# Own trigger points and a sixth buffer for the loads of summed weight tiles

## The chip, the core and the metric

The kernel runs on one core of one Trainium2 chip. The metric is the device time of one launch in microseconds (us). The engines are named as in the profile: PE is TensorE, DVE is VectorE, ACT is ScalarE, POOL is GpSimd and SP is SyncE; PEld is the weight load of PE. A "q" behind an engine (SPq) marks its queue of instructions.

## What is computed

The reference is a decoder trunk of two layers on a sequence of 512 tokens of width 1024. The change concerns the MLP at the end of each layer:

```python
h2 = rms_norm(x, norm2_g[l])
x = x + jnp.square(jax.nn.relu(h2 @ w_up[l])) @ w_down[l]
```

`w_up` is 1024 x 4096 and `w_down` is 4096 x 1024, both float32. In front of it, each layer has a gated recurrence, a windowed attention in three groups and an output projection, which the change doesn't touch.

## The kernel before

**Weights.** All weights of a layer lie in one array of 148 tiles of 128 x 1024 float32 (512 KB), in the order of their use. Each tile is loaded and split into a high part `wH` (ACT, line 112) and the rest `wL` (DVE, line 113), and a product takes three matmuls: high by high, high by low, low by high. `plan` (line 54) writes the list of the tiles in the order of their products. `weight` (line 123) keeps three split tiles in a queue: before it hands one out it calls `prep` (line 81) for the tile two places further on. `prep` runs at high priority. `wH` and `wL` have three buffers each, so a split waits until the product of three tiles before is done. The framework orders each engine's instructions when the program is compiled, and that order is then fixed; semaphores hold an instruction back until its data and its buffer are there.

**The MLP.** For each quarter of the 4096 inner columns (q = 0 to 3), `up` (line 667) computes eight products with plain ("raw") tiles, of 24 matmuls of 512 columns each; `operands` (line 599) then forms seven combinations of the squared results. The product with `w_down` is done by `seven` (line 610) in two groups (g = 0, 1) per quarter. A group replaces eight products of blocks by seven, whose weights are sums of blocks. So a layer has eight groups and the kernel sixteen; each has seven tiles of 24 matmuls of 256 columns (line 631), 168 in all. The first product of the next quarter stands ahead of group 0, its other seven behind group 1, so that the two groups of a quarter follow each other without a pause. After each product `take` adds the accumulator to `x` on DVE (line 638), and later products of the group write the same accumulator again.

**The tiles of a group.** `groups` in `plan` lists seven items. With w0 to w3 for the four blocks:

- x11: f11 = w0, a plain load; split
- s1: f1 = w2, a load on SP (line 104), to which a DMA of POOL then adds w3 in place (line 105); split
- s2: f2 = f1 + f11, an addition on DVE (line 107); split
- s4: f12 = w1, a load (line 110), and f4 = f2 + f12 on DVE (line 111); split
- s3: f3 = w0, a load, to which POOL adds w2 in place; split
- x12: f12 again; split
- raw: w3, a load into the buffers of the raw tiles; split

The tiles f11, f1, f2, f4, f12 and f3 share one tag "f" with five buffers. The buffers go round in the order in which the tiles are made in the program: the n-th tile takes the buffer of the tile five places earlier and waits until that one has been read for the last time. A load is part of `prep` of its own item.

Of the kernel before, what the change touches and what calls it, by code (L numbers as in the profile page):

```python
# [8 lines left out]
F32 = mybir.dt.float32  # L9
# [3 lines left out]
OP = mybir.AluOpType  # L13

P = 128
S = 512
D = 1024
KD = 8
# [5 lines left out]
NW = 148  # L24
# [4 lines left out]
class Trunk:  # L29
# [24 lines left out]
    def plan(self):  # L54
        items = []
        for l in range(DEPTH):
            at = l * NW
            plain = lambda n: [("raw", l, at - l * NW + i) for i in range(n)]

            def take(n):  # L60
                nonlocal at
                got = plain(n)
                at += n
                return got

            def groups():
                nonlocal at
                got = []
                for g in range(2):
                    i = at - l * NW  # L70
                    got += [("x11", l, i), ("s1", l, i + 2, i + 3), ("s2",), ("s4", l, i + 1),
                            ("s3", l, i, i + 2), ("x12",), ("raw", l, i + 3)]
                    at += 4
                return got

            items += take(NW - 64 + KD + 1) + groups()
            for q in (1, 2):
                items += take(KD) + groups()
            items += take(KD - 1) + groups()
        self.items = items  # L80

    def sum_tile(self):
        return self.mp.tile([P, 1024], F32, tag="f", name=self.nm("f"), bufs=5)

    def prep(self, urgent=True):
        nc = self.nc
        kind, *at = self.items[self.wi]
        self.wi += 1
        with self.tc.high_priority() if urgent else nullcontext():
            if kind == "x12":  # L90
                raw = self.f12
            elif kind == "raw":
                raw = self.wp.tile([P, 1024], F32, tag="raw", name=self.nm("raw"), bufs=2)
            else:
                raw = self.sum_tile()
            h = self.wp.tile([P, 1024], F32R, tag="wH", name=self.nm("wH"), bufs=3)
            lo = self.wp.tile([P, 1024], F32R, tag="wL", name=self.nm("wL"), bufs=3)
            n = 1024 // self.parts
            for c in range(self.parts):
                cs = slice(c * n, (c + 1) * n)  # L100
                if kind in ("raw", "x11"):
                    nc.sync.dma_start(raw[:, cs], self.w[at[0], at[1], :, cs])
                elif kind in ("s1", "s3"):
                    nc.sync.dma_start(raw, self.w[at[0], at[1]])
                    nc.gpsimd.dma_start(raw, self.w[at[0], at[2]], accum_op=OP.add)
                elif kind == "s2":
                    nc.vector.tensor_add(raw, self.f1, self.f11)
                elif kind == "s4":
                    self.f12 = self.sum_tile()
                    nc.sync.dma_start(self.f12, self.w[at[0], at[1]])  # L110
                    nc.vector.tensor_add(raw, self.f2, self.f12)
                nc.scalar.activation(h[:, cs], raw[:, cs], AF.Copy)  # L112
                nc.vector.tensor_sub(lo[:, cs], raw[:, cs], h[:, cs].bitcast(F32))  # L113
            self.parts = 1
        if kind == "x11":
            self.f11 = raw
        elif kind == "s1":
            self.f1 = raw
        elif kind == "s2":
            self.f2 = raw  # L120
        self.wq.append((h, lo))

    def weight(self):
# [584 lines left out]
    def finish(self, x, xp, cs):  # L708
        nc = self.nc
        bc = self.bcast(self.stats([self.ssq[:, cs], self.sq]))  # L710
        rb = xp.tile([P, 256], F32, tag="rbf", name=self.nm("rbf"), bufs=2)
        nc.scalar.activation(rb, bc, AF.Copy)
        for k in range(KD):
            if k < 2:
                nc.gpsimd.tensor_mul(x[:, k, cs], x[:, k, cs], rb)
            else:
                nc.vector.tensor_mul(x[:, k, cs], x[:, k, cs], bc)
        for a, b in ((2, 4), (4, 6), (0, 2), (6, 8)):
            (nc.sync if a % 4 else nc.scalar).dma_start(self.outT[a:b, :, cs].rearrange("k p t -> p k t"), x[:, a:b, cs])
# [19 lines left out]
    def run(self):  # L739
        nc, tc = self.nc, self.tc  # L740
        with ExitStack() as es:
# [4 lines left out]
            self.mm = es.enter_context(tc.tile_pool(name="mmps", bufs=4, space=bass.MemoryType.PSUM))  # L746
            self.ax = es.enter_context(tc.tile_pool(name="axps", bufs=2, space=bass.MemoryType.PSUM))
            self.hx = es.enter_context(tc.tile_pool(name="hxps", bufs=2, space=bass.MemoryType.PSUM))
            self.wi, self.wq, self.parts = 0, [], 4
            self.plan()  # L750

            def open_x(name):
                xs = ExitStack()
                xp = xs.enter_context(tc.tile_pool(name=name, bufs=1, side="right", reuse_waits="tile"))
                return xp.tile([P, KD, S], F32, name=name + "_t"), xp, xs
# [5 lines left out]
            x, xp, xs = open_x("x_in")  # L761
# [39 lines left out]
            for l in range(DEPTH):  # L801
                with ExitStack() as ms:
                    pool = lambda st, name, bufs, side="left": st.enter_context(tc.tile_pool(
                        name=f"{name}{l}", bufs=bufs, side=side, reuse_waits="tile"))
# [45 lines left out]
                    x, xp, xs = open_x(f"x{l}")  # L850
# [11 lines left out]
                    rb = xp.tile([P, S], F32, name=self.nm("rb"))  # L862
# [127 lines left out]
```

## Time and profile before

| | |
|---|---|
| runs shown | 1811.43, 1815.75, 1817.28 us; median 1815.75 |
| profiled execution | 1819.03 us, of which the span from the first to the last instruction is 1817.1 |
| busy in the span | PE 98%, PEld 84%, DVE 62%, ACT 40%, POOL 5% |
| granted clock of PE | mean 0.992 of full speed |
| DMA | 199 MB, mean 110 GB/s |

The profile is of one execution, and its times are counted from the start of the span. "Busy" counts the time in which an engine has an instruction running. Matmuls overlap each other in the pipeline, so PE can be busy and yet below its best pace; the length of a stretch with a known number of matmuls tells more than its busy time. An idle time in brackets behind an instruction stands ahead of it and names who ended it.

### The profile page before, as it was taken

How to read it: one execution, taken by the hardware profiler on the slowest of the kernel's cores; microseconds unless marked ns; L12 is line 12 of the kernel's file. 1: busy time of each engine (PE TensorE's matmuls, PEld its weight loads, DVE VectorE, ACT ScalarE, POOL GpSimd, SP SyncE). 2: the span in 40 equal slices, each digit the busy share in tenths (PEclk: the TensorE clock that was granted, in tenths of full speed). 3: DMA queues.
4: the chain of work that ended last, by engine and by line, in shares of the span. 5: the costliest groups of instructions: out<-in, count | busy, mean ns of one | idle time of the engine just before them, and what ended most of it. 6: DMA issues, size and time to landing. Idle time of an engine off the chain costs nothing.

```text
span 1817.1 us, 23831 instructions
## 1 busy us (share of the span) xinstructions
PE 1774.6 (98%) x9428; PEld 1532.8 (84%) x9428; DVE 1125.4 (62%) x1964; ACT 727.1 (40%) x1093; POOL 83.7 (5%) x127
## 2 busy tenths in 40 slices
PE   8999999999999999999999999999999999999897
PEld 6888888888888989888988889888888889898887
DVE  7676553564556666667877764545545566666666
ACT  6354223342344343433553443234333443434244
POOL 2000000000000000000100000000000000000000
PEclk9999999999999999999999999999999999999999
DMA  5221333323324535353441223333232345354542
GB/s 175 82 66 51 113 102 106 104 92 102 96 93 139 145 123 136 119 139 117 133 132 60 70 76 96 108 102 100 70 128 93 114 128 152 118 145 122 130 127 81
DMA packets 58367, 199.14 MB, mean 110 GB/s; under 512 B 7376, under 2 KB 10192, under 8 KB 58256
## 3 DMA queue, kind: packets, MB, share of 16 engines
q1 hardware_dynamic: 48176, 167.85, 28.2%
q0 software_dynamic: 8992, 28.72, 8.1%
q8 instruction: 74, 1.21, 0.3%
q10 hardware_dynamic: 1088, 1.05, 0.2%
q14 instruction: 37, 0.30, 0.1%
HBM read 187.83 MB, written 4.26 MB: 106 GB/s over the span
## 4 chain that ended last, share of the span: by engine, by line
PE 85%; DMA 7%; DVE 4%; issue 2%; ACT 2%; SPq 0%; DVEq 0%; POOLq 0%; ACTq 0%
PE mm L134 19%; PE mm L136 19%; PE mm L135 19%; DMA f<-in_w 6%; PE mm L631 5%; PE mm L156 3%; PE mm L157 3%; PE mm L158 3%; DVE wL L113 2%; PE hx L322 2%; PE hx L631 2%; PE hx L564 2%; PE ax L631 2%; ACT wH L112 1%; PE ax L478 1%
## 5 line engine op out<-in xcount | busy, mean ns | idle before, releaser
L134 PE MATMUL mm<-hH,wH 128*128 128x512 f32 x1344 | 530.2, 395 | 5.8 <-ACT hH L235 5.7
L136 PE MATMUL mm<-hH,wL 128*128 128x512 f32 x1344 | 531.5, 396 | 0.3 <-DVE wL L113 0.3
L135 PE MATMUL mm<-hL,wH 128*128 128x512 f32 x1344 | 527.3, 393 | 1.6 <-DVE hL L236 1.6
L112 ACT ACTIVATE wH<-raw 128x1024 fp32r<-128x1024 f32 (+1 forms) x251 | 263.0, 1049 | 534.8 <-PE mm L135 291.3
L113 DVE TENSOR_TENSOR wL<-raw,wH 128x1024 fp32r<-128x1024 f32 (+1 forms) x251 | 303.2, 1208 | 123.4 <-ACT wH L112 122.9
L134 PEld LDWEIGHTS mm<-hH,wH 128*128 128x128 f32 x1344 | 253.4, 189 | 57.6 <-ACT hH L235 7.5
L135 PEld LDWEIGHTS mm<-hL,wH 128*128 128x128 f32 x1344 | 253.1, 188 | 56.0 <-DVE hL L236 4.6
L136 PEld LDWEIGHTS mm<-hH,wL 128*128 128x128 f32 x1344 | 253.3, 188 | 51.3 <-DVE wL L113 0.8
L112 ACT ACTIVATE wH<-f 128x1024 fp32r<-128x1024 f32 x96 | 100.8, 1056 | 157.2 <-PE mm L631 65.8
L631 PE MATMUL mm<-aH,wH 128*128 128x256 f32 x512 | 148.4, 291 | 14.5 <-DVE x_t L638 14.5
L113 DVE TENSOR_TENSOR wL<-f,wH 128x1024 fp32r<-128x1024 f32 x96 | 117.3, 1222 | 50.1 <-ACT wH L112 49.7
L631 PE MATMUL mm<-aL,wH 128*128 128x256 f32 x512 | 147.5, 288 | 0.0
L631 PE MATMUL mm<-aH,wL 128*128 128x256 f32 x512 | 147.3, 288 | 0.0
L631 PEld LDWEIGHTS mm<-aH,wH 128*128 128x128 f32 x512 | 100.9, 197 | 17.5 <-ACT wH L112 13.1
L156 PE MATMUL mm<-wH,hH 128*128 128x512 f32 x256 | 104.6, 409 | 0.0
L158 PE MATMUL mm<-wH,hL 128*128 128x512 f32 x256 | 104.4, 408 | 0.0
L157 PE MATMUL mm<-wL,hH 128*128 128x512 f32 x256 | 103.0, 402 | 0.0
L631 PEld LDWEIGHTS mm<-aL,wH 128*128 128x128 f32 x512 | 101.0, 197 | 0.3
L631 PEld LDWEIGHTS mm<-aH,wL 128*128 128x128 f32 x512 | 100.9, 197 | 0.0
L674 DVE SCALAR_TENSOR_TENSOR r<-mm,rb 128x512 f32<-128x512 f32 x64 | 43.8, 687 | 60.1 <-PE mm L136 60.0
L486 ACT ACTIVATE P<-P,negm 128x128 f32<-128x128 f32 (+1 forms) x96 | 39.9, 417 | 81.9 <-DVE negm L483 81.9
L631 PE MATMUL ax<-aH,wH 128*128 128x256 f32 x256 | 72.4, 284 | 0.2 <-DVE x_t L638 0.2
(249 smaller groups left out, 2645.7 us busy)
## 6 DMA issues: line engine op xcount, KB each, us to landing
raw<-in_w SPq DMA_DIRECT2D x247, 512.0 KB, 3.5
f<-in_w SPq DMA_DIRECT2D x64, 512.0 KB, 4.4
f<-in_w POOLq DMA_DIRECT2D x32, 512.0 KB, 5.5
qk<-qk POOLq DMA_DIRECT2D x42, 128.0 KB, 2.2
x_in_t<-in_xT SPq DMA_DIRECT2D x8, 256.0 KB, 6.1
x_t<-in_xT POOLq DMA_DIRECT2D x8, 256.0 KB, 5.0
x_mid<-x_t POOLq DMA_DIRECT2D x8, 256.0 KB, 4.1
x_t<-x_mid POOLq DMA_DIRECT2D x8, 256.0 KB, 4.6
```

The source lines that it names most:

```text
L112: nc.scalar.activation(h[:, cs], raw[:, cs], AF.Copy)
L113: nc.vector.tensor_sub(lo[:, cs], raw[:, cs], h[:, cs].bitcast(F32))
L134: nc.tensor.matmul(ps, wH(i), aH(k), start=s, stop=False)
L135: nc.tensor.matmul(ps, wH(i), aL(k), start=False, stop=False)
L136: nc.tensor.matmul(ps, wL(i), aH(k), start=False, stop=e)
L156: nc.tensor.matmul(ps[tb], a, mH, start=(k == 0), stop=False)
L157: nc.tensor.matmul(ps[tb], a, mL, start=False, stop=False)
L158: nc.tensor.matmul(ps[tb], b, mH, start=False, stop=(k == KD - 1))
L322: nc.tensor.matmul(pv[:, c], k[:, cc * P:(cc + 1) * P], R[:, cc], start=True, stop=True)
L486: nc.scalar.activation(Pt[:, j, lo:], Pt[:, j, lo:], AF.Exp, bias=nm[:, j:j + 1], scale=SCALE, accum_out=Dn[:, j, hd:hd + 1])
L631: ins = nc.tensor.matmul(ps, wt[:, p, m], av[:, m, slot], start=first and m == 0 and j == 0, stop=m == 3 and j == 2, skip_group_check=True)
L674: nc.vector.scalar_tensor_tensor(v, ps, 0.0, rb, op0=OP.max, op1=OP.mult)
```

## The change

Each item of the list now has three parts: its kind, its place in the weights or the two tiles that it sums, and a list of loads ("fetches") that are issued after the item has been prepared. `prep` of a summed item only splits what is there, or adds two tiles on DVE and splits the sum. `fetch` makes the tile, issues the load on SP and, where there is a second block, the accumulating DMA on POOL. It is called behind the block of high priority.

The fetches hang on these items: f12 on f11, f3 on f1, and both f11 and f1 of the next group on f2 of this group. Those of a layer's first group hang on the fifth item ahead of it. The tag "f" has six buffers in place of five. `finish` puts its factors into the two tiles "wv" and "wy" of the x pool, which `wide_rstd` has used, in place of two tiles of its own. What is added, split and multiplied stays the same, and so does the number of DMAs.

```diff
                 for g in range(2):
                     i = at - l * NW
-                    got += [("x11", l, i), ("s1", l, i + 2, i + 3), ("s2",), ("s4", l, i + 1),
-                            ("s3", l, i, i + 2), ("x12",), ("raw", l, i + 3)]
+                    nxt.append([("f11", (l, i)), ("f1", (l, i + 2), (l, i + 3))])
+                    after = []
+                    got += [("f11", None, [("f12", (l, i + 1))]), ("f1", None, [("f3", (l, i), (l, i + 2))]),
+                            ("f2", ("f1", "f11"), after), ("f4", ("f2", "f12"), []), ("f3", None, []),
+                            ("f12", None, []), ("raw", (l, i + 3), [])]
+                    slots.append(after)
                     at += 4
...
+            slots = []
+            first = take(NW - 64 + KD + 1)
+            slots.append(first[-KD + 3][2])
+            items += first + groups()
...
+            for s, n in zip(slots, nxt):
+                s += n
...
-    def sum_tile(self):
-        return self.mp.tile([P, 1024], F32, tag="f", name=self.nm("f"), bufs=5)
+    def fetch(self, name, at, more=None):
+        nc = self.nc
+        t = self.F[name] = self.mp.tile([P, 1024], F32, tag="f", name=self.nm("f"), bufs=6)
+        nc.sync.dma_start(t, self.w[at[0], at[1]])
+        if more:
+            nc.gpsimd.dma_start(t, self.w[more[0], more[1]], accum_op=OP.add)
...
-                elif kind in ("s1", "s3"):
-                    nc.sync.dma_start(raw, self.w[at[0], at[1]])
-                    nc.gpsimd.dma_start(raw, self.w[at[0], at[2]], accum_op=OP.add)
-                elif kind == "s2":
-                    nc.vector.tensor_add(raw, self.f1, self.f11)
-                elif kind == "s4":
-                    self.f12 = self.sum_tile()
-                    nc.sync.dma_start(self.f12, self.w[at[0], at[1]])
-                    nc.vector.tensor_add(raw, self.f2, self.f12)
...
+            elif at:
+                raw = self.F[kind] = self.mp.tile([P, 1024], F32, tag="f", name=self.nm("f"), bufs=6)
+                nc.vector.tensor_add(raw, self.F[at[0]], self.F[at[1]])
...
+            for f in fetches:
+                self.fetch(*f)
...
-        rb = xp.tile([P, 256], F32, tag="rbf", name=self.nm("rbf"), bufs=2)
+        rb = xp.tile([P, S], F32, tag="wy" if cs.start else "wv", name=self.nm("rbf"))[:, :256]
```

## Rows read from the trace of the kernel before

**Rows 1.** The head of the page and its part 1, busy time.

```profile
span 1817.1 us, 23831 instructions
PE 1774.6 (98%) x9428; PEld 1532.8 (84%) x9428; DVE 1125.4 (62%) x1964; ACT 727.1 (40%) x1093; POOL 83.7 (5%) x127
```

**Rows 2.** Waits of PE: engine, product, who was waited for: us, times, longest.

```profile
PE mm L631 <- DVE x_t L638: 14.5, 14, 2.5
PE hx L631 <- DVE wL L113: 8.2, 5, 2.2
```

**Rows 3.** Six first groups, q 0 to 2: length, busy, PEclk, DMA share, GB/s.

```profile
603.59:624.19 20.60, 20.38 (x169) 20.20 (x168) 16.29 (x23) 8.04 (x9) 0.85 (x1) 1.00 0.52 137
691.69:715.71 24.02, 21.90 (x170) 21.69 (x168) 16.85 (x24) 8.04 (x9) 0.86 (x1) 0.93 0.47 124
...
1674.80:1698.85 24.05, 21.89 (x169) 21.68 (x168) 16.88 (x24) 8.04 (x9) 0.86 (x1) 0.93 0.50 120
sum 131.13, PE 125.38 PEld 124.23 DVE 98.89 ACT 48.24 POOL 5.14; mean PE 20.90 PEld 20.70 DVE 16.48 ACT 8.04 POOL 0.86
```

**Rows 4.** The four others of these six alone, which start at 603.59, 783.12, 1499.06, 1586.28.

```profile
sum 83.06, PE 81.59 PEld 80.85 DVE 65.15 ACT 32.17 POOL 3.42; mean PE 20.40 PEld 20.21 DVE 16.29 ACT 8.04 POOL 0.85
```

**Rows 5.** The six second groups of q 0 to 2, in the same columns.

```profile
624.19:648.14 23.95, 21.80 (x170) 21.63 (x169) 14.79 (x24) 6.87 (x7) 1.70 (x2) 0.93 0.67 170
...
1519.86:1542.73 22.87, 20.57 (x170) 20.27 (x169) 14.74 (x24) 6.13 (x6) 1.73 (x2) 1.00 0.63 161
...
sum 142.19, PE 128.70 PEld 127.16 DVE 88.18 ACT 39.61 POOL 10.31; mean PE 21.45 PEld 21.19 DVE 14.70 ACT 6.60 POOL 1.72
```

**Rows 6.** The four groups of the last quarters (q 3) of both layers, summed.

```profile
sum 87.79, PE 83.85 PEld 82.14 DVE 73.38 ACT 49.80 POOL 8.23; mean PE 20.96 PEld 20.54 DVE 18.34 ACT 12.45 POOL 2.06
```

**Rows 7.** Timelines of five engines, 621 to 639 us: start, length, what [idle before].

```profile
621.35 1.22 DVE L113 TENSOR_TENSOR wL<-f,wH 128x1024 fp32r<-128x1024 f32 x1
622.59 0.33 SPq L104 DMA_DIRECT2D f<-in_w  x1
627.39 0.85 POOL L105 DMA_DIRECT2D f<-in_w  x1 [16.40 <-DVE x_t L638]
635.23 2.00 ACT L112 ACTIVATE wH<-f 128x1024 fp32r<-128x1024 f32 x2 [7.02 <-DMA f<-in_w]
636.32 1.23 DVE L113 TENSOR_TENSOR wL<-f,wH 128x1024 fp32r<-128x1024 f32 x1 [5.75 <-ACT wH L112]
638.02 0.55 PE L631 MATMUL mm<-aH,wH 128*128 128x256 f32 x1 [2.15 <-DVE x_t L638]
```

**Rows 8.** The 3.2 us behind that stall, in the columns of rows 3.

```profile
638.02:641.20 3.18, 3.18 (x15) 3.18 (x16) 3.18 (x6) 0.16 (x1) 0.00 (x0) 0.50 0.50 165
```

**Rows 9.** Timelines of DVE, ACT and SP where buffers come free, 599 to 628 us.

```profile
599.22 1.23 DVE L113 TENSOR_TENSOR wL<-f,wH 128x1024 fp32r<-128x1024 f32 x1 [0.18 <-ACT wH L112]
606.23 0.33 SPq L104 DMA_DIRECT2D f<-in_w  x1
610.51 1.23 DVE L113 TENSOR_TENSOR wL<-f,wH 128x1024 fp32r<-128x1024 f32 x1 [0.55 <-ACT wH L112]
627.15 1.06 ACT L112 ACTIVATE wH<-f 128x1024 fp32r<-128x1024 f32 x1 [1.82 <-PE mm L631]
```

**Rows 10.** The additions f2 = f1 + f11 on DVE: two of them, and who ended the idle time.

```profile
615.48 1.23 DVE L107 TENSOR_TENSOR f<-f,f 128x1024 f32<-128x1024 f32 x1 [2.63 <-DMA f<-in_w]
706.19 1.23 DVE L107 TENSOR_TENSOR f<-f,f 128x1024 f32<-128x1024 f32 x1 [5.25 <-DMA f<-in_w]
  DMA f<-in_w: 29.0, 10
```

**Rows 11.** Part 6 of the page (count, KB, us to landing), and one issue of SP.

```profile
f<-in_w SPq DMA_DIRECT2D x64, 512.0 KB, 4.4
f<-in_w POOLq DMA_DIRECT2D x32, 512.0 KB, 5.5
694.32 0.33 SPq L104 DMA_DIRECT2D f<-in_w  x1
```

More of the change, by code (lines that the diff above doesn't have):

```diff
@@ L57, in plan @@
             at = l * NW
-            plain = lambda n: [("raw", l, at - l * NW + i) for i in range(n)]
+            nxt = []
             def take(n):
                 nonlocal at
-                got = plain(n)
+                i = at - l * NW
                 at += n
-                return got
+                return [("raw", (l, i + j), []) for j in range(n)]
             def groups():
@@ L70, in groups @@
                     i = at - l * NW
-                    got += [("x11", l, i), ("s1", l, i + 2, i + 3), ("s2",), ("s4", l, i + 1),
-                            ("s3", l, i, i + 2), ("x12",), ("raw", l, i + 3)]
+                    nxt.append([("f11", (l, i)), ("f1", (l, i + 2), (l, i + 3))])
[4 more added lines that the diff above has]
+                    slots.append(after)
                     at += 4
                 return got
-            items += take(NW - 64 + KD + 1) + groups()
+            slots = []
+            first = take(NW - 64 + KD + 1)
+            slots.append(first[-KD + 3][2])
+            items += first + groups()
             for q in (1, 2):
@@ L79, in plan @@
             items += take(KD - 1) + groups()
+            for s, n in zip(slots, nxt):
+                s += n
         self.items = items
-    def sum_tile(self):
-        return self.mp.tile([P, 1024], F32, tag="f", name=self.nm("f"), bufs=5)
+    def fetch(self, name, at, more=None):
[4 more added lines that the diff above has]
+            nc.gpsimd.dma_start(t, self.w[more[0], more[1]], accum_op=OP.add)
     def prep(self, urgent=True):
         nc = self.nc
-        kind, *at = self.items[self.wi]
+        kind, at, fetches = self.items[self.wi]
         self.wi += 1
         with self.tc.high_priority() if urgent else nullcontext():
-            if kind == "x12":
-                raw = self.f12
-            elif kind == "raw":
+            if kind == "raw":
                 raw = self.wp.tile([P, 1024], F32, tag="raw", name=self.nm("raw"), bufs=2)
+            elif at:
+                raw = self.F[kind] = self.mp.tile([P, 1024], F32, tag="f", name=self.nm("f"), bufs=6)
+                nc.vector.tensor_add(raw, self.F[at[0]], self.F[at[1]])
             else:
-                raw = self.sum_tile()
+                raw = self.F[kind]
             h = self.wp.tile([P, 1024], F32R, tag="wH", name=self.nm("wH"), bufs=3)
@@ L100, in prep @@
                 cs = slice(c * n, (c + 1) * n)
-                if kind in ("raw", "x11"):
+                if kind == "raw":
                     nc.sync.dma_start(raw[:, cs], self.w[at[0], at[1], :, cs])
-                elif kind in ("s1", "s3"):
-                    nc.sync.dma_start(raw, self.w[at[0], at[1]])
-                    nc.gpsimd.dma_start(raw, self.w[at[0], at[2]], accum_op=OP.add)
-                elif kind == "s2":
-                    nc.vector.tensor_add(raw, self.f1, self.f11)
-                elif kind == "s4":
-                    self.f12 = self.sum_tile()
-                    nc.sync.dma_start(self.f12, self.w[at[0], at[1]])
-                    nc.vector.tensor_add(raw, self.f2, self.f12)
                 nc.scalar.activation(h[:, cs], raw[:, cs], AF.Copy)
@@ L114, in prep @@
             self.parts = 1
[L115 to L120, printed above, removed]
+            for f in fetches:
+                self.fetch(*f)
         self.wq.append((h, lo))
@@ L748, in run @@
             self.hx = es.enter_context(tc.tile_pool(name="hxps", bufs=2, space=bass.MemoryType.PSUM))
-            self.wi, self.wq, self.parts = 0, [], 4
+            self.wi, self.wq, self.parts, self.F = 0, [], 4, {}
             self.plan()
```

## The prediction

> **What bounds the kernel now.** I first read the head of the page: PE is busy for 1774.6 of 1817.1 us [rows 1], so only its idle time and its slow stretches can be gained, and DVE, at 62%, has room on the average. Second, who PE waits for: at line 631, the products of `seven`, it waits 14.5 us for DVE's additions into `x` and 8.2 us for a split [rows 2]; these are most of its idle time of 42.5 us. Third, the length of each of the sixteen groups, which all have 168 matmuls. Four of the six first groups of q 0 to 2 take 83.06 / 4 = 20.77 us [rows 4], which I take as an undisturbed group; the other two take 24.02 and 24.05 [rows 3]. The six second groups take 142.19 us, 23.70 each [rows 5]. The four groups of the last quarters take 87.79 us, 21.95 each [rows 6]. So the second groups lose 142.19 - 6 x 20.77 = 17.6 us, and two first groups lose 6.5 us together: 24.1 us in twelve groups.
>
> Fourth, one second group step by step. At 621.35 DVE splits f11 and its buffer is free at 622.57; at 622.59 SP issues the load of f3 into it; at 627.39 POOL issues the accumulation; ACT gets the data at 635.23, after 7.02 us of idleness; DVE stood for 5.75 us at this split, with the additions into `x` queued behind it, and PE stood 2.15 us for one of those [rows 7]. So the tile took 12.64 us from its buffer to its data. ACT's turn for it would have come at 627.15 + 2.88 = 630.03, as ACT prepares a tile per product [rows 9], and an undisturbed product takes 24 x 0.12 = 2.88 us. The load came 5 us too late because of its buffer. The stall costs twice: behind it PE was granted 0.50 of its clock (1.2 in place of 2.4 GHz) for 3.2 us, in which 15 matmuls ran [rows 8]; at 0.12 us each they take 1.8 us, so 1.4 us more are lost. The windows with 0.93 in the clock's column are those in which that happened; 1519.86 has the stall alone, 22.87 us [rows 3, 5].
>
> The same hold appears in the first groups at the addition f2 = f1 + f11: DVE waits for f1's data, 29.0 us over 10 of 16 additions. Where it waited 2.63 us, the group took 20.60; where it waited 5.25, it took 24.02 [rows 3, 10]. A wait of under 3 us is thus hidden by what PE has queued, and one of over 5 is not.
>
> **The change, part by part.** Removed: nothing that is computed. Loads, additions, splits and matmuls are as many as before, so 64 + 32 DMAs of 512 KB and DVE's 16.3 us of a 20.77 us group stay [rows 4, 11].
>
> *Buffers.* In program order a group now makes f12, f3, f2, f11', f1', f4 (a dash marks the next group), six tiles, and the ring has six buffers. So each tile takes the buffer of the tile of its own name one group back, and its load can start when that one has been split, if nothing ahead of it on SP holds it. For f3 that is the end of the split of the previous f3: 610.51 + 1.23 = 611.74 [rows 9] against 622.59 [rows 7], 10.85 us earlier. With the same 12.64 us the data is there at 624.4, 5.6 us ahead of ACT's turn at 630.0. DVE's stand of 5.75 us and PE's of 2.15 go, with the half clock behind it. For f1 of a second group it is the end of the split of f1 (599.22 + 1.23 = 600.45) in place of that of f2 (606.23) [rows 9], 5.8 us earlier; behind another group only one tile, some 2.9 us. f12 and f11 are plain loads (4.4 us) and have several tiles' time.
>
> *What is late next.* The addition f2. The compiler has placed it in DVE's queue ahead of its data: DVE reached it 2.63 to 5.25 us too soon [rows 10]. Now it may also be placed earlier, as f1's load is, and then the wait stays, in second groups too, where the stand at f3 used to cover it. A wait of 2.63 us costs nothing beyond 20.77, as the undisturbed groups hold just that. I therefore bound a group by 20.77 us below and by 24.03, the mean of the two bad first groups, above. For first groups I take 20.77, as f1 there gains 5.8 us. For second groups, where f1 gains less and its accumulation meets the load of the next f3, I take 21.3, nearer to the lower end as the load still leads by a tile.
>
> *Moved DMAs.* The loads leave the high priority. On SP only loads of raw tiles and of "f" tiles stand; a fetch that waits for its buffer holds back a raw load behind it by at most one tile's split. On POOL an accumulation waits for its base load, and behind it stand the next accumulation and, in the last quarter of layer 0, stores of `x`; these have no consumer near. I cost both at nothing: raw loads are issued a buffer ahead; if that cover is gone, each late raw tile costs up to its load, about the 4.4 us of its likes [rows 11].
>
> *finish.* "wv" and "wy" were last read before the MLP, so its factors wait for nothing: 0 us, below or above by no more than one ACT instruction of 256 columns, which isn't seen here (at most the 1.06 us of one of 1024 columns [rows 9]).
>
> *Last quarters.* DVE is busy for 18.34 of 21.95 us there [rows 6], with the next norm's work; between a gain of 4 x (21.95 - 20.77) = 4.7 us and none I take none, since that work stays.
>
> *Sum.* First groups 131.13 - 6 x 20.77 = 6.5 us; second groups 142.19 - 6 x 21.3 = 14.4 us; together 20.9 us. The profiled execution took 1819.03 us (span 1817.1 and 1.9 around it), so 1798.1 after. It lies 3.3 us above the median of the runs, 1815.75, so I predict 1795.
>
> **Rivals.**
>
> *The wait moves to f2 (slower).* If the addition is placed as far ahead of f1's data in every group as in the two bad ones, all twelve take 24.03: 288.4 against 273.3 us, 15 us slower, 1831. It decides where the wait at f2 passes some 3 us. For it speaks that chains to f2 differ much: 9.25 us (606.23 to 615.48) and 11.87 (694.32 to 706.19) [rows 9 to 11], and that more loads are now in flight together. Against it speaks that f1's load starts earlier in all groups and that f3's load is out of its way in most.
>
> The Trainium skill ("DMA: Bandwidth & Descriptors", section "Issuing engines are not separate DMA queues") speaks for this rival: DMAs that SP and POOL issue run on the same engines and interleave, so loads issued earlier together stretch each other. The trace of before doesn't part such transfers from lone ones, so no row here shows it apart. By this rule alone f1 would arrive later than I say, and the time would be the 1831 above.
>
> *Partly: waits of about 4 us at f2 in second groups.* Between 2.63 us (20.77) and 5.25 (24.03) that is 20.77 + 3.26 x 1.37 / 2.62 = 22.5 a group; first groups stay as they are. Gain 142.19 - 135.0 = 7.2 us: 1809.
>
> *The loads don't start earlier.* The fetch of f3 stands in the program behind the splitting of f1, three items ahead of its use. If the compiler leaves it there on SP, it is issued at the start of the product ahead of the group, about 1.35 us before 622.59 [rows 7]: the stand of 5.75 us becomes 4.4, a second group takes 20.77 + 3.26 x (4.4 - 2.63) / 2.62 = 23.0, and 4 to 5 us are gained: 1811. Against it: SP has nothing else to wait for there, and before it issued a load 0.02 us after its buffer came free [rows 7].
>
> **How the numbers follow.** Forecast 0.57 (1788 to 1803: all twelve groups between 20.77 and 22.0, and a little from the last quarters); the partial case 0.17; no earlier loads 0.15; the wait at f2 0.11. Differences within 0.3% (5.4 us) can't be told from none by a measurement of this kernel. Faster is forecast and partial case, 0.74; same is the third rival, 0.15; slower is the first, 0.11. The range goes from 1788, the low end of the forecast, to 1812, which takes in the partial case and the third rival and leaves out the slower one.
>
> **What would show it.** The six second groups at 20.8 to 22 us, without windows of half clock; no stand of 5 us at the split of f3; the load of f3 issued some 10 us earlier, just behind the split of the f3 before; waits at the addition of f2 of under 3 us. I am wrong if DVE's waits for the addition grow past 3 us in second groups, if raw loads land late in `up`, or if the sixth buffer moves other tiles so that the MLP starts later.

## The result and the profile after

| | before | after |
|---|---|---|
| median, us | 1815.93 | 1783.32 (1783.15 to 1783.87) |
| ratio | | 0.9825, interval 0.9808 to 0.9842 |
| span of the profiled execution | 1817.1 | 1781.6 |
| the six first groups of q 0 to 2 | 131.13 | 120.93 |
| the six second groups of q 0 to 2 | 142.19 | 120.96 |
| the four groups of the last quarters | 87.79 | 83.66 |

The change makes the kernel 1.75% faster, 32.6 us of the median. The prediction was 1795, with a range from 1788 to 1812: the sign was right, and the gain is larger than the range allowed.

The head of the page and part 1, against [rows 1]: the span is 35.5 us shorter and PE is busy for 99% of it. The instructions of every engine are as many as before, and only the busy times of PE and PEld fall much, by 12.5 and 9.4 us.

```profile
span 1781.6 us, 23821 instructions
PE 1762.1 (99%) x9428; PEld 1523.4 (86%) x9428; DVE 1128.4 (63%) x1964; ACT 728.2 (41%) x1093; POOL 83.7 (5%) x127
```

Busy time by stretch: a first and a second group of q 0, the sum over all twelve groups of q 0 to 2, then the sum over the four of the last quarters; columns as in [rows 3].

```profile
603.77:623.93 20.16, 20.16 (x170) 20.15 (x169) 16.37 (x25) 8.87 (x9) 0.85 (x1) 1.00 0.63 176
623.93:644.09 20.16, 20.16 (x171) 20.16 (x170) 14.98 (x22) 7.42 (x7) 1.70 (x2) 1.00 0.66 183
...
sum 241.89, PE 241.89 PEld 241.87 DVE 184.46 ACT 95.83 POOL 15.42; mean PE 20.16 PEld 20.16 DVE 15.37 ACT 7.99 POOL 1.29
...
sum 83.66, PE 83.09 PEld 82.01 DVE 73.65 ACT 49.80 POOL 6.45; mean PE 20.77 PEld 20.50 DVE 18.41 ACT 12.45 POOL 1.61
```

The reader sees twelve equal groups: 20.16 us is 168 matmuls at 0.12 us, so PE is never held, and the clock's column is 1.00 in each. Against [rows 3, 5, 6] the groups give back 10.2, 21.2 and 4.1 us, together 35.6: this is the whole difference of the spans. Everything outside `seven` is as long as before.

PE's waits: the longest in total, the one at line 632 for DVE, and the one for a split (against [rows 2]; line 631 of before is line 632 here, and 638 is 639):

```profile
PE mm L135 <- ACT hH L236: 5.7, 2, 5.5
...
PE mm L632 <- DVE x_t L639: 0.5, 3, 0.2
...
PE mm L137 <- DVE wL L118: 0.3, 1, 0.3
```

The 14.5 us for the additions into `x` are 0.5, and the 8.2 us for a split in `seven` have gone. What is left longest, 5.7 us at line 135, lies outside the MLP's groups.

The loads. Timelines of DVE, SP and POOL from 596 to 634 us, the same place as [rows 7, 9]: start, length, what [idle before].

```profile
596.68 0.33 SPq L94 DMA_DIRECT2D f<-in_w  x1
604.84 1.23 DVE L118 TENSOR_TENSOR wL<-f,wH 128x1024 fp32r<-128x1024 f32 x1 [0.17 <-ACT wH L117]
606.09 0.33 SPq L94 DMA_DIRECT2D f<-in_w  x1
607.82 1.23 DVE L118 TENSOR_TENSOR wL<-f,wH 128x1024 fp32r<-128x1024 f32 x1
609.07 0.33 SPq L94 DMA_DIRECT2D f<-in_w  x1
610.70 1.23 DVE L118 TENSOR_TENSOR wL<-f,wH 128x1024 fp32r<-128x1024 f32 x1 [0.55 <-ACT wH L117]
612.17 1.22 DVE L107 TENSOR_TENSOR f<-f,f 128x1024 f32<-128x1024 f32 x1
...
619.34 1.23 DVE L118 TENSOR_TENSOR wL<-f,wH 128x1024 fp32r<-128x1024 f32 x1 [0.55 <-ACT wH L117]
620.59 0.33 SPq L94 DMA_DIRECT2D f<-in_w  x1
624.84 0.85 POOL L96 DMA_DIRECT2D f<-in_w  x1 [9.68 <-DMA f<-in_w]
630.91 1.22 DVE L118 TENSOR_TENSOR wL<-f,wH 128x1024 fp32r<-128x1024 f32 x1 [0.60 <-ACT wH L117]
632.38 1.22 DVE L107 TENSOR_TENSOR f<-f,f 128x1024 f32<-128x1024 f32 x1
```

A dash marks the next group's tile, two dashes the one after. In order: f1' is loaded at 596.68; the split of f2 ends at 606.07 and f12' is loaded at 606.09; the split of f4 ends at 609.05 and f3' is loaded at 609.07, 13.5 us earlier than the 622.59 of [rows 7]; the split of f3 ends at 611.93 and the addition that makes f2' begins at 612.17; the split of f11' ends at 620.57 and f1'' is loaded at 620.59. The accumulation of f1'' starts at 624.84 and lands at 630.38, and the addition f2'' that reads it starts 2.0 us later, at 632.38, behind the split of f3' (ends 632.13). No bracket stands behind either addition: in the groups DVE doesn't wait for f1 any more [rows 10]. Two additions f2 still wait, 4.49 and 3.29 us, each ahead of a layer's first group (568.15 and 1443.56), where PE is at the products of `up` and no wait of PE for them shows.

Part 6 of the page, against [rows 11]: as many loads, 4.1 us in place of 4.4, and the accumulations as long as before. The transfers themselves are hardly faster; they start earlier.

```profile
f<-in_w SPq DMA_DIRECT2D x64, 512.0 KB, 4.1
f<-in_w POOLq DMA_DIRECT2D x32, 512.0 KB, 5.5
```

### The profile page after: what moved, and what is told of

It reads as the page before. It is cut to its first block, busy times and chain, and to the rows that moved or that the text cites. A ratio compares the mean times of both kernels' runs of the same rounds, so it can differ in the third digit from the quotient of the medians.

```text
span 1781.6 us, 23821 instructions
## 1 busy us (share of the span) xinstructions
PE 1762.1 (99%) x9428; PEld 1523.4 (86%) x9428; DVE 1128.4 (63%) x1964; ACT 728.2 (41%) x1093; POOL 83.7 (5%) x127
## 3 DMA queue, kind: packets, MB, share of 16 engines
q1 hardware_dynamic: 48176, 167.85, 28.6%
## 4 chain that ended last, share of the span: by engine, by line
PE 95%; DVE 2%; issue 1%; ACT 1%; DMA 1%; SPq 0%; DVEq 0%; POOLq 0%
PE mm L135 20%; PE mm L137 20%; PE mm L136 20%; PE mm L632 10%; PE ax L632 5%; PE mm L157 3%; PE mm L158 3%; PE mm L159 3%; PE hx L632 3%; PE hx L323 2%; PE hx L565 2%; PE ax L479 1%; PE ax L469 1%; PE ax L554 1%; PE hx L368 1%
## 5 line engine op out<-in xcount | busy, mean ns | idle before, releaser
L632 PE MATMUL mm<-aH,wH 128*128 128x256 f32 x512 | 144.6, 283 | 0.5 <-DVE x_t L639 0.5
L632 PE MATMUL ax<-aL,wH 128*128 128x256 f32 x256 | 72.4, 283 | 0.0
```

What stands on the lines that cost most here:

```text
L632: ins = nc.tensor.matmul(ps, wt[:, p, m], av[:, m, slot], start=first and m == 0 and j == 0, stop=m == 3 and j == 2, skip_group_check=True)
```

## Experiments

Three things are mixed in the change: the sixth buffer, the trigger points of the loads within a group (f12, f3), and those of the next group (f11, f1). Theory A: the trigger points, above all the order in which tiles are made and so get their buffers, carry the gain; the sixth buffer only makes an order possible. Theory B: the sixth buffer carries it.

### Six buffers, old loads

The kernel before with one buffer more (and the change of `finish`, which frees the memory for it).

```diff
-        return self.mp.tile([P, 1024], F32, tag="f", name=self.nm("f"), bufs=5)
+        return self.mp.tile([P, 1024], F32, tag="f", name=self.nm("f"), bufs=6)
```

> The kernel before with six buffers for the tag f in place of five (and the change's finish, which makes the room); every load stays in the preparation of its own item. Theory A (what the change brings is the order in which tiles are made, which decides which buffer each load and each addition takes): the load of f3 in a second group now starts at the end of the split of f12 of the first group, in time, so the 5 us stand at f3 goes; but f1's load starts at the split of the previous f1 and the addition f2 is queued on DVE right behind the additions of the first product, before the data: DVE is held 2.5 to 5 us in every group. About 1.5 us are lost in each of twelve groups: 1800, from 1793 to 1808. Theory B (the sixth buffer alone does it): 1783 to 1786, with no hold at f2.

Measured: 1846.26 us, 1.0175 of before (1.0150 to 1.0199), slower. Theory B falls; A expected a gain and had the sign wrong here. Two of the six second groups with their sum, in the columns of [rows 3], and then a load of f1, its accumulation and the addition f2, in the timelines:

```profile
624.75:652.16 27.41, 22.07 (x171) 21.90 (x170) 14.25 (x22) 7.41 (x7) 1.70 (x2) 0.88 0.58 144
716.52:743.58 27.06, 22.65 (x171) 22.48 (x170) 15.31 (x22) 7.41 (x7) 1.72 (x2) 0.87 0.59 155
...
sum 163.92, PE 134.92 PEld 133.88 DVE 90.30 ACT 44.47 POOL 10.28; mean PE 22.49 PEld 22.31 DVE 15.05 ACT 7.41 POOL 1.71
```

```profile
714.49 0.86 POOL L105 DMA_DIRECT2D f<-in_w  x1 [17.00 <-DVE x_t L638]
716.07 0.33 SPq L104 DMA_DIRECT2D f<-in_w  x1
724.01 0.86 POOL L105 DMA_DIRECT2D f<-in_w  x1 [8.67 <-DMA f<-in_w]
729.77 1.23 DVE L107 TENSOR_TENSOR f<-f,f 128x1024 f32<-128x1024 f32 x1 [6.87 <-DMA f<-in_w]
```

f1's load goes out at 716.07, 1.6 us behind the accumulation of f3, and takes 7.39 us beside it; its own accumulation then lands at 729.69. DVE has reached the addition 6.87 us before, and PE stands 4.4 us for the additions into `x` behind it; then come 3.4 us of half clock. In the six second groups DVE's wait there is 6.9 to 7.8 us. The data of f1 is hardly earlier in the group than before (13.2 us behind its start here, 14.1 in the group of before that starts at 715.71), but DVE is at the addition 6.4 us behind the start, where the stand at f3 held it to 13.8. Of the 28.6 us between the profiled spans the second groups lose 21.7 and the last quarters 12.7, and the first groups gain 5.9. This is the slower rival of the prediction, the wait that moves to f2, in a kernel where only the buffers were added (and `finish` changed).

### Own triggers with five buffers

With five buffers the next group's loads can't hang on f2: f12, f3, f2, f11' and f1' would hold all five, and f4 could not be made. They hang on f4 here, so the kernel after that, with six buffers and the same trigger, is its counterpart.

```diff
-                            ("f2", ("f1", "f11"), after), ("f4", ("f2", "f12"), []), ("f3", None, []),
+                            ("f2", ("f1", "f11"), []), ("f4", ("f2", "f12"), after), ("f3", None, []),
...
-        t = self.F[name] = self.mp.tile([P, 1024], F32, tag="f", name=self.nm("f"), bufs=6)
+        t = self.F[name] = self.mp.tile([P, 1024], F32, tag="f", name=self.nm("f"), bufs=5)
```

In the first of these kernels the tag "q" of the recurrence went from six buffers to five too, by an oversight; the second has it at six.

> The changed kernel with five buffers; so that they suffice, the loads of the next group's f11 and f1 hang on f4 and not on f2. Theory A: a buffer for f3 comes free at the split of the previous f3, early enough; the load of f1 starts one to two tiles later than in the changed kernel, and the addition f2 waits for the buffer of f12, so its data is 0 to 3 us late. Holds of DVE of under 2.2 us cost nothing: 1784 to 1793, most likely 1787. Theory B (the sixth buffer does it): near the kernel before, 1805 to 1816.

> The run with five buffers again, now with the tag f alone changed: in the first one a tag of the recurrence, q, had lost a buffer too. The groups should be as there (second groups near 21.6 us on the average, with holds of DVE at the addition f2 of 1 to 6 us): 1793 to 1797. If the loss there came from q: 1783.

Measured: 1795.18 us (0.9893, 0.9870 to 0.9916) and 1794.86 (0.9893, 0.9862 to 0.9924). The oversight made no difference that can be seen. The first time lies between the two theories' ranges, 2 us above that of A. Two thirds of the gain are there without the sixth buffer. What is missing stands in single groups; one of the second groups of the second kernel, and the sum of the six:

```profile
621.78:645.44 23.66, 21.45 (x170) 21.27 (x169) 13.96 (x22) 6.35 (x6) 1.70 (x2) 0.95 0.71 180
...
sum 127.96, PE 123.96 PEld 123.61 DVE 81.01 ACT 39.04 POOL 10.29; mean PE 20.66 PEld 20.60 DVE 13.50 ACT 6.51 POOL 1.71
```

In each of the six the addition f2 waits for f1's data, 1.8 to 2.0 us in four, which cost nothing (20.16 us each), and 5.11 and 4.68 us in the two of 23.66. One group of the last quarters is 24.96 us long; PE waits 3.08 us in it, as in the kernel with the other order of the loads, below.

### Six buffers, next loads on f4

```diff
-                            ("f2", ("f1", "f11"), after), ("f4", ("f2", "f12"), []), ("f3", None, []),
+                            ("f2", ("f1", "f11"), []), ("f4", ("f2", "f12"), after), ("f3", None, []),
```

> The same with six buffers: the partner of the run with five, and the changed kernel with the two loads of the next group hung on f4 in place of f2. Theory A: f1 of a first group's successor is loaded at the split of the previous f1, the addition f2 waits for the buffer of f3 and finds its data; behind second groups its data comes 0 to 3 us after DVE reaches it. 1783 to 1787. Theory B: as the changed kernel, 1783, and some 20 to 30 us faster than the run with five. If what matters is only where a load hangs in the program: slower than the changed kernel by a tile's time per group, 2.9 us x 16, 1830.

Measured: 1783.08 us (0.9831, 0.9809 to 0.9852), as after. With the same trigger, the sixth buffer is worth 1794.86 - 1783.08 = 11.8 us. But its margin is gone: the addition of f2 waits for its data again in all second groups, 1.1 to 2.2 us in five, and in the sixth 4.55 us, which cost 22.08 - 20.16 = 1.92 us. That group and its addition:

```profile
1668.26:1690.34 22.08, 20.55 (x170) 20.25 (x169) 14.02 (x21) 6.36 (x6) 1.72 (x2) 1.00 0.59 147
```

```profile
1681.30 1.23 DVE L107 TENSOR_TENSOR f<-f,f 128x1024 f32<-128x1024 f32 x1 [4.55 <-issue]
```

### f3's load hung on f2

A later trigger for f3, together with the next group's loads, but ahead of them.

```diff
-                    after = []
-                    got += [("f11", None, [("f12", (l, i + 1))]), ("f1", None, [("f3", (l, i), (l, i + 2))]),
+                    after = [("f3", (l, i), (l, i + 2))]
+                    got += [("f11", None, [("f12", (l, i + 1))]), ("f1", None, []),
```

> The changed kernel with the load of f3 hung on f2 in place of f1, so that it is made after f2's tile. Theory A: f2 then takes the buffer of f4, one tile earlier, and its addition stands earlier on DVE (just behind the split of f4); f3 takes the buffer of the previous f3. DVE waits about 1 us at the addition behind second groups, not at all in first groups; PE hides it: 1783 to 1785. If f3's lead is what carries the gain: f3 is loaded 2.9 us later than in the changed kernel and still lands some 5 us ahead of its turn, so no difference either; a time over 1790 would speak against both.

Measured: 1795.31 us (0.9893, 0.9867 to 0.9919). I had expected no change. One of the six second groups and their sum, then, in that group, the accumulation of f1, the next load on SP and the addition f2:

```profile
707.50:728.70 21.20, 20.50 (x170) 20.26 (x169) 13.69 (x21) 6.37 (x7) 1.72 (x2) 1.00 0.57 139
...
sum 126.73, PE 122.34 PEld 121.38 DVE 82.60 ACT 39.37 POOL 10.30; mean PE 20.39 PEld 20.23 DVE 13.77 ACT 6.56 POOL 1.72
```

```profile
709.35 0.86 POOL L96 DMA_DIRECT2D f<-in_w  x1 [8.94 <-DVE x_t L639]
709.98 0.33 SPq L94 DMA_DIRECT2D f<-in_w  x1
716.83 1.22 DVE L107 TENSOR_TENSOR f<-f,f 128x1024 f32<-128x1024 f32 x1 [3.67 <-issue]
```

f1's accumulation at 709.35 has a load of SP 0.63 us behind it, takes 7.40 us and lands at 716.75; the addition starts 0.08 us later. (The bracket names "issue", since DVE's wait is recorded as an instruction of its own.) In the kernel after, the same accumulation at the same place of the group (708.38) has the load 1.88 us behind it and takes 5.37. Of f1's accumulations in this kernel's six second groups, those with a load issued within 1.0 us on either side took 7.01 to 7.40 us in four cases and 5.60 in one; the one with the load 1.34 us behind took 5.37. So an accumulation that is issued together with a load takes longer, here by about 2 us on 5.4. The Trainium skill ("DMA: Bandwidth & Descriptors", section "Issuing engines are not separate DMA queues") says that what different engines issue runs on the same DMA engines and interleaves; with that rule these times agree. The lateness of the data is one part of the wait. The other is that DVE reaches the addition earlier, 5.7 us into this group (713.16) against 8.45 in after, since f2 has the buffer of f4 here. The last quarters, 89.45 us against 83.66, make up the other half of the loss; what holds them stays open.

### The order of the next loads, with five buffers

The second kernel with five buffers, but f1 of the next group is made ahead of f11, and so takes a buffer one tile earlier.

```diff
-                    nxt.append([("f11", (l, i)), ("f1", (l, i + 2), (l, i + 3))])
+                    nxt.append([("f1", (l, i + 2), (l, i + 3)), ("f11", (l, i))])
```

> As the run before it, five buffers and the next group's loads on f4, but with f1 made ahead of f11, so that f1 takes the buffer that comes free a tile earlier. Theory A (what costs is the hold of DVE at f2, when f1's chain of load and accumulation lands after DVE reaches the addition; the order of the tiles decides both): f1 starts 2.9 us or more earlier, the addition still waits for the buffer of f12, so the holds of 5 us shrink to under 2.6 us, which cost nothing: 1784 to 1790 with what the last quarter leaves. Theory B (own triggers need the sixth buffer): 1793 to 1797 as with the other order.

Measured: 1786.40 us (0.9846, 0.9827 to 0.9864), 8.5 us less than with the other order. One second group and the sum of the six:

```profile
707.30:727.46 20.16, 20.16 (x171) 20.16 (x169) 13.23 (x20) 6.36 (x6) 1.72 (x2) 1.00 0.72 198
...
sum 120.96, PE 120.96 PEld 120.96 DVE 82.43 ACT 42.89 POOL 10.29; mean PE 20.16 PEld 20.16 DVE 13.74 ACT 7.15 POOL 1.71
```

f1's data is there 0.6 to 1.5 us ahead of the addition in all six, and no group is longer than PE's pace. The order of the tiles does in these groups what the sixth buffer does in the change. What is left, 3.1 us, is nearly all one group of the last quarters (23.46 us), in which PE waits 3.1 us for an addition into `x`. No load is late there: DVE works without a pause from 871.33 us to the addition at 878.53, on three splits and on work of the next norm (lines 237 and 206), which stand ahead of the addition in its queue. The addition starts 8.4 us behind the group's start; in after the additions into `x` at this place start 5.3 us behind it (875.85). Why the compiler orders them so stays open.

### f3's load alone

The kernel before, in which only the load of f3 is issued with the preparation of f1, three items earlier; with five buffers, and with six.

```diff
+            if kind == "s1":
+                self.f3 = self.sum_tile()
+                nc.sync.dma_start(self.f3, self.w[at[0], at[1] - 2])
+                nc.gpsimd.dma_start(self.f3, self.w[at[0], at[1]], accum_op=OP.add)
```

> The kernel before with one load moved: f3 is made and loaded in the preparation of s1, behind f1, with the five buffers of before. Theory A: f3's data is there in time in second groups, so the stand of over 5 us at its split goes; but f1 of the next group now starts at the split of f2 and meets f3's load, so DVE is held at the addition f2, by 3 to 7 us behind second groups and 2 to 5 in first ones: 1795 to 1812, most likely 1802. If the late f3 alone is what the change removes: 1795 or less, with no hold over 3 us.

> The same with six buffers. Theory A: the addition f2 is queued on DVE earlier (a buffer is there for it), and f1's load starts at the split of the previous f1, a tile ahead of f3's, which it then meets: holds of 4 to 6 us at f2 behind second groups, about 4 us lost in each with the half clock: 1795 to 1820, most likely 1807. If a sixth buffer helps a load that has its own trigger: faster than the run with five, 1785 to 1795.

Measured: 1809.98 us (0.9968, 0.9953 to 0.9983) and 1815.01 (0.9992, 0.9975 to 1.0009). DVE's waits for the data of f1 at the addition f2 and of f12 at f4: the first row is of the kernel with five buffers, the other two of the one with six; columns as in [rows 2].

```profile
DVE f L109 <- DMA f<-in_w: 52.6, 14, 5.3
```

```profile
DVE f L109 <- DMA f<-in_w: 31.3, 8, 5.3
DVE f L113 <- DMA f<-in_w: 30.7, 16, 4.3
```

The stall at f3 has gone in both, but DVE now waits at 14 of the 16 additions f2, 52.6 us against 29.0 over 10 [rows 10]; with six buffers, part of it moves on to f4. Half clock falls in four and five of the groups. So the step on which I built most of the forecast, f3's load, is worth 6 us or nothing by itself: the load of the tile next in need comes too late then. The opposite, the next group's loads moved and f3's left where it was, wasn't run, so how the gain divides between the trigger points isn't shown.

### f1 loaded twice

To see what margin the change has at f2: the base block of f1 is loaded twice, which puts its accumulation one load (about 4 us) later. The result is the same.

```diff
         nc.sync.dma_start(t, self.w[at[0], at[1]])
+        if more and name == "f1":
+            nc.sync.dma_start(t, self.w[at[0], at[1]])
```

> The changed kernel, in which the base block of f1 is loaded twice, one load behind the other, before the accumulation: f1's data is some 4.5 us later, DVE's queue stays as it is. Theory A: in second groups f1 lands about 10.5 to 12 us into the group, and DVE reaches the addition at 8.45: a hold of 2 to 3.6 us, of which the products hide 2.6; up to 1 us is lost in each of six groups, some more where SP's other loads are pushed back: 1784 to 1792. If the change has brought f1 so early that 4.5 us don't matter: 1783. If each us of delay is a us of time: 16 x 4.5 us, 1855.

Measured: 1791.88 us (0.9867, 0.9841 to 0.9893), 8.6 us more than after. Two second groups, and the timeline around the addition in the second:

```profile
710.41:730.57 20.16, 20.16 (x171) 20.16 (x170) 13.96 (x21) 6.37 (x6) 1.72 (x2) 1.00 0.74 207
...
1588.77:1614.78 26.01, 23.11 (x171) 22.91 (x169) 14.98 (x22) 7.42 (x7) 1.73 (x2) 0.87 0.59 163
```

```profile
1593.68 0.86 POOL L98 DMA_DIRECT2D f<-in_w  x1 [14.95 <-DMA f<-in_w]
1594.12 0.33 SPq L94 DMA_DIRECT2D f<-in_w  x1
1603.17 1.23 DVE L109 TENSOR_TENSOR f<-f,f 128x1024 f32<-128x1024 f32 x1 [5.87 <-issue]
```

Here the accumulation meets a load 0.44 us behind it and takes 9.41 us; in the other two long groups it takes 8.07 and 8.47, and DVE waits 3.97 and 5.25 us. In the three second groups where the load is 1.23 to 1.28 us behind, it takes 5.33 to 5.65, DVE waits 1.0 to 1.3 us, and the group stays at 20.16. So 4 us of delay alone are nearly covered by the margin, and what costs is the delay together with the meeting.

### f1 ahead of f11 with six buffers, loaded once and twice

The kernel after with the order of the next loads turned round as above, and the same with f1's base block loaded twice.

> The changed kernel with six buffers and the load of f1 made ahead of that of f11: f1 then takes the buffer of f12, two tiles earlier. Theory A: the groups run at PE's pace already, so nothing is gained: 1782 to 1785. If the last quarters still wait for f1: up to 1 us faster.

> Both: f1 ahead of f11, and its base block loaded twice. Theory A: the lead of two tiles, 5.8 us, takes up the 4.5 us of the second load, so no hold over 2.6 us: 1782 to 1786. If the second load costs by the transfers that it adds and not by f1's lateness: as the run with f11 ahead.

Measured: 1784.41 us (0.9831, 0.9811 to 0.9851) and 1783.24 (0.9824, 0.9800 to 0.9848). Neither differs from after by what can be told. The twelve groups of q 0 to 2 of the second kernel, summed:

```profile
sum 241.89, PE 241.89 PEld 241.87 DVE 182.87 ACT 94.78 POOL 15.42; mean PE 20.16 PEld 20.16 DVE 15.24 ACT 7.90 POOL 1.29
```

In the first, f1's data is there 3.2 to 4.8 us ahead of the addition in the six second groups, against 1.6 to 2.5 in after, and only two first groups are longer than 20.16 us (20.95 and 20.67). With the second load that lead is used up, and all twelve groups are at PE's pace. The extra 4 us cost 8.6 us in the order of the change and nothing in this one. So it isn't the added transfers that cost; what decides is when f1's accumulation lands against the addition. No version ran measurably faster than after.

## Why the prediction was right in sign and too small

**What bounds the kernel, and where the gain lies: right.** All of it came out of the sixteen groups, PE's waits at line 631 went from 14.5 and 8.2 us to 0.5 and nothing, and no half clock is left in the groups. The step that failed is the price of DVE's wait at the addition f2: the sum let that wait stand in all twelve groups of q 0 to 2, in the first ones hidden in the floor, and in after it is gone. Of the 35.5 us the sum had 20.9; three terms lack 14.6 us, the first two by this step:

- *The undisturbed group, 20.77 us.* I took the four best first groups for the floor. They held the wait of 2.63 us and its like at f2 themselves. The floor is 168 x 0.12 = 20.16, and I had the 0.12 in hand, for a product of 24. 12 x 0.61 = 7.3 us.
- *Second groups, 21.3 us.* 0.53 us each for a wait at f2 that was to stay: 6 x 0.53 = 3.2 us. There was none.
- *Last quarters, none.* 4.1 us: of the ends 4.7 and none I took the wrong one. DVE's work there is as much as before (73.65 us, before 73.38 [rows 6]) and wasn't the bound.

Together 14.6.

**"A wait of 2.63 us costs nothing": wrong by a part.** The rows of before give it: the groups with 2.63 to 2.95 us of waiting are 0.44 to 0.75 us longer than 20.16. In the kernels with own triggers a group's loss is its wait less 2.6 to 2.7 us, wherever the clock held: waits of 3.67, 3.99 and 4.99 us (f3 hung on f2) cost 1.04, 1.37 and 2.37; 4.55 (next loads on f4) costs 1.92; 3.97 and 5.25 (f1 twice) cost 1.26 and 2.54. Waits of up to 2.31 us cost nothing. So the cover is some 2.2 us in the kernel before and 2.6 to 2.7 in these, and then each us costs one; I had drawn a line from 20.77 at 2.63 to 24.03 at 5.25, which mixes in the half clock.

**The ring of buffers: wrong.** I said that a tile takes the buffer of the tile of its own name one group back. The timeline above shows that each takes the one that comes free next, in the order in which the compiled program first writes the tiles: f3' goes out behind the split of f4 (609.07), not behind that of f3 (611.74 by my sum). For the kernel before both readings give the same, so its rows couldn't tell them apart. The loads are thus earlier than I had them: f3' by 13.5 us, not 10.85; f1' at 596.68 against 606.23 [rows 9], 9.6 us, not 5.8.

**"The wait at f2 stays": wrong, by the same cause.** The sum f2 takes a buffer too, and it is the one that f3 leaves (611.93, addition at 612.17). So the addition can't run before the end of that split, and by then f1's data is there: 606.04 for f2', 6.1 us before; 630.38 for f2'', 2.0 us before. I expected the addition to move up with f1's load; the buffer keeps it back. Two runs, of which this was said beforehand, bear it out: with f3 hung on f2 the sum takes the buffer of f4, and the addition in the first group stands right behind the split of f4 (its end 608.76, the addition 609.01); with five buffers and f1 ahead it takes that of f12 and stands behind that split (614.37, 614.61). No run moves the buffer of f2 and nothing else.

**The slower rival: not in this kernel, but real.** Its mechanism is the first experiment: 7 us of waiting at f2, second groups of 27.3 us, more than the 24.03 I gave it. Its point of decision lies near: the kernel after has 1.6 to 2.5 us of margin, and 4 us more on f1's path bring the waits back. What keeps it off is the buffer of f2, which the prediction didn't see; that the change came out faster in spite of it was luck in this point. The other two rivals fell: the fetch of f3 isn't held by the splitting of f1, and waits of 4 us at f2 don't appear in the groups of after.

**"The trace of before doesn't part such transfers from lone ones": wrong.** It does. Nine of its 32 accumulations have a load of SP issued between 1.30 us ahead of them and 0.66 behind, and took 6.89 to 7.74 us; of the other 23, nineteen took 5.25 to 5.69. The accumulation of f3 in the step-by-step group (627.39, 7.74 us) is one of the nine, so the 12.64 us of its chain hold such a meeting. The price of the first rival could have been worked out from these rows.

**The moved DMAs: right in their price, wrong in a detail.** No raw tile came late: PE's wait for a split is 0.3 us in all. But the statement, in the section on the change and in the prediction, that the fetches stand behind the block of high priority is wrong: in the code they are called within it. Compiled with them outside, the kernel has the same instructions in the same order on all five engines, so nothing of the result hangs on this. *finish* cost nothing that shows: the spans outside the groups are as before.

## What to carry to other kernels

Take the floor of a repeated stage from the work counted (matmuls times their pace), not from the best of its repetitions, which may all hold the same wait. Where loads are made earlier, follow every tile of the shared buffers in the order in which the compiled program writes them, additions too, and ask for each whose last read sets it free: six buffers alone cost 31 us here, and with five the order of two loads was worth 8. A load that a stall names need not be the only late one: f3's, moved alone, handed the wait to f1's.

## What the runs showed that I hadn't expected

- f1's accumulating DMA of 512 KB took 5.29 to 5.54 us in the second groups of after, where the next load follows it by 1.0 to 1.9 us. Where a load is issued closer to it, it mostly took 7.0 to 9.4: 8.07, 8.47 and 9.41 us (f1 twice, loads 0.99, 0.12 and 0.44 us behind), 7.01 to 7.40 (f3 on f2). Near 1 us it goes either way: f3's in after took 5.93 and 5.63 with loads 0.82 and 0.93 us behind, but 8.63 with one 0.60 behind. A shift of a trigger by 1 us can so cost 2 to 4 us until the data lands.
- A sixth buffer made the kernel before slower by 31 us. It lets f1's load out earlier, but beside another accumulation, so that its data comes hardly earlier; and DVE, no longer held at f3, is at the addition some 7 us earlier and waits there.
